# Moving the output products of a chunked scan into the next chunk, and the wide products that fill it into two places instead of three

## The chip, the cores and the metric

The kernel runs on one core of a Trainium2 chip. The metric is the device time of one execution in microseconds (us); 0.2% of it is 2.4 us. The engines are called as in the profile: PE (matrix products), PEld (the loading of the stationary operand for PE), DVE (VectorE), ACT (ScalarE), POOL (GpSimd) and SP (which here only issues DMAs). Each engine takes its instructions in the order in which the program put them into its queue.

## The reference, cut to what matters

One layer works on 512 tokens of width 1024, all in float32: a gated feed-forward half step, two token mixers side by side, a gated merge, a second half step and a last norm.

```python
x = x + 0.5 * swiglu(rms_norm(x, ffn1_norm), ffn1_w1, ffn1_w3, ffn1_w2)
p = rms_norm(x, mix_norm) @ w_in                    # columns of both mixers and of the two gates
y_a = rwkv7_mixer(token_shift(p[..., :SHIFT_COLS])) @ rwkv_proj
y_b = fox_mixer(p[..., SHIFT_COLS:SHIFT_COLS + FOX_COLS]) @ fox_proj
x = x + (sigmoid(g_a) * y_a + sigmoid(g_b) * y_b) @ w_out
x = x + 0.5 * swiglu(rms_norm(x, ffn2_norm), ffn2_w1, ffn2_w3, ffn2_w2)
out = rms_norm(x, final_norm)

def step(state, inp):                               # inside rwkv7_mixer: 8 heads of 64, over all 512 tokens
    r_t, w_t, k_t, v_t, a_t, b_t = inp
    sa = einsum('bhvk,bhk->bhv', state, a_t)
    state = state * w_t[:, :, None, :] + sa[..., :, None] * b_t[:, :, None, :] + v_t[..., :, None] * k_t[:, :, None, :]
    return state, einsum('bhvk,bhk->bhv', state, r_t)
```

The recurrence `step` is the part that the change is about. The second mixer, `fox_mixer`, is causal attention of 8 heads with a decay in its logits.

## The kernel before, in words

**Wide products.** A float32 weight tile is cut into a high and a low part: ACT casts the high part (L122, `whi`), DVE subtracts (L123, `wlo`). Each product with a 128 by 512 activation then takes three instructions on PE (L130, L131, L132). These "wide products" fill the two feed-forward blocks and the projections. A column of `w_in` takes 8 such triples, 24 instructions.

**The scan.** The recurrence is worked off in 16 chunks of 32 tokens (`NC` = 16). `step(p)` has prepared, per pair of heads, tiles `G` (decayed readers of the state), `BK` (writers) and, with a triangular inverse, `Tb`. A chunk `c` then has these parts, all small:
- `xps` (L781, 8 products): the state is read, in `R = Rs[c % 4]`. DVE copies the result to `Xs` (L784).
- `ups` (L788, 4 products): `Xs` through the chunk's inverse. ACT copies the result into `R`, four copies (L790, L791).
- `sps` (L795, 8 products): the new state from `R` and `Dt`. DVE multiplies by the decay into the next chunk's `Rn` (L797, two instructions). This ends the chain that chunk `c + 1` waits for.
- `yps` (L806, 8 products): the chunk's outputs, from `R` and `G`. ACT copies them to `V4` (L807). No later chunk needs them.
- every second chunk, `stage(c + 2)` brings in operands for two chunks: transposes `vp` and `bp` on PE, eight copies on ACT (L769, L770).

Each of the 8 products is two instructions in the trace.

**What fills the gaps.** Between dependent parts of a chunk PE has to wait for DVE or ACT. The list `holes` names, for successive triples of wide products, the small product behind which they are placed: `holes += [hx, hx, hu, hu, hs, hs]` puts two triples (six wide instructions) behind `xps`, two behind `ups` and two behind `sps`. The method `cols` takes its places from this list; the triples are those of the attention's query and key columns (`load_qk(2)` and `(3)`, tile `pq`) and of nine gate columns (`early`, tile `pgt`). `tc.issue_after` is the tool: it says that an instruction has to stand behind another on its queue.

**Attention.** It is written after the scan in the program and runs beside it: norms of queries and keys (`norm_qk`: L712, L142, L143, then PE L148 with tile `pq`, then L718, L719, L720), parts of queries and keys (L844 to L850), logits `lp` (L862 to L864), softmax (L870 to L876), transposes (L880, L882), products with values (L891, L893).

**What sets the order.** The order on every queue is made by a scheduler that plays the program through with its own costs when it is built. It moves whatever no `issue_after` or dependence holds. So a changed place on PE also changes the order on ACT, DVE, POOL and SP.

**Buffers.** `xps`, `yps`, `ups`, `sps`, `vp` and `bp` share three PSUM buffers in turn (pool `pr`). A new one of them can be written only when the one three places before it has been copied out.

Of the kernel before, what the change touches and what calls it, by code (L numbers as in the profile page):

```python
# [9 lines left out]
F32 = mybir.dt.float32  # L10
# [8 lines left out]
P = 128  # L19
# [6 lines left out]
NP = DA // P  # L26
C = 32
NC = T // C
# [23 lines left out]
def kernel(  # L52
# [7 lines left out]
    dve, act, pool, pe = nc.vector, nc.scalar, nc.gpsimd, nc.tensor  # L60
# [6 lines left out]
    pr = ctx.enter_context(tc.tile_pool(name="pr", bufs=3, space=PSUM))  # L67
# [358 lines left out]
    with ExitStack() as mx:  # L426
        rp = mx.enter_context(tc.tile_pool(name="rp", bufs=1))
        holes = []
        sctx = ExitStack()
        sp = sctx.enter_context(tc.tile_pool(name="sp", bufs=1))  # L430
        G = [[sp.tile([P, NC, 2, C], F32, name=f"G{p}{q}", tag=f"G{p}{q}") for q in range(2)] for p in range(NP)]
# [81 lines left out]
        V4 = rp.tile([P, NP, T], F32, name="V4", tag="V4")  # L513
# [149 lines left out]
        Tb = Tall[:].rearrange("p (a c t) -> p a c t", a=2, c=NC)  # L663
# [7 lines left out]
        def heads():  # L671
            return [(p, q) for p in range(NP) for q in range(2)]

        def half(q):
            return slice(q * 64, (q + 1) * 64)
# [72 lines left out]
        Rs, Ds = [RD[i // 2][:, i % 2] for i in range(4)], [RD[2 + i // 2][:, i % 2] for i in range(4)]  # L748
# [8 lines left out]
        def stage(c):  # L757
            vp = pr.tile([P, NP, 2, 64], F32, tag="b", name="vp")
            for p in range(NP):
                pe.transpose(vp[0:64, p].rearrange("p a b -> p (a b)"), vs[p][:, c * C:(c + 2) * C], ident[:])  # L760
            bp = pr.tile([P, NP, 2, 64], F32, tag="b", name="bp")
            for p in range(NP):
                pe.transpose(bp[:, p].rearrange("p a b -> p (a b)"),
                             BKs[p][:, c:c + 2].rearrange("p c a b -> p (c a b)"), ident[:])
            for j in range(2):
                Rj, Dj = Rs[(c + j) % 4], Ds[(c + j) % 4]
                for q in range(2):
                    o = 32 + (1 - q) * 64
                    act.copy(Rj[o:o + 32, :, q, :], vp[j * C:(j + 1) * C, :, q, :])  # L769
                    act.copy(Dj[half(1 - q), :, q, :], bp[half(j), :, q, :])  # L770

        stage(0)

        for c in range(NC):
            R, Rn, Dt = Rs[c % 4], Rs[(c + 1) % 4], Ds[c % 4]
            cs = slice(c * C, (c + 1) * C)
            xps = pr.tile([P, 2, 64], F32, tag="b", name="xps")
            for p, q in heads():
                o = (p // 2) * 64 + q * C
                with tc.issue_after(ahead.ins):  # L780
                    hx = pe.matmul(xps[o:o + C, p % 2, :], G[p][q][:, c, 0, :], R[:, p, q, :], start=True, stop=True,  # L781
                                   tile_position=(0, o))
            Xs = sp.tile([P, 2, 64], F32, tag="Xs", name="Xs", bufs=2)
            dve.tensor_copy(Xs[:], xps[:])  # L784
            ups = pr.tile([P, 2, 64], F32, tag="b", name="ups")
            for p in range(NP):
                h = half(p // 2)
                hu = pe.matmul(ups[h, p % 2, :], Tb[h, p % 2, c, :], Xs[h, p % 2, :], start=True, stop=True)  # L788
            for i in range(2):
                act.copy(R[64:96, 2 * i:2 * i + 2, 0, :], ups[64 * i:64 * i + 32])  # L790
                act.copy(R[0:32, 2 * i:2 * i + 2, 1, :], ups[64 * i + 32:64 * i + 64])  # L791
            if c + 1 < NC:
                sps = pr.tile([P, NP, 64], F32, tag="b", name="sps")
                for p, q in heads():
                    hs = pe.matmul(sps[half(q), p, :], Dt[:, p, q, :], R[:, p, q, :], start=True, stop=True)  # L795
                for q in range(2):
                    decay = dve.tensor_tensor(Rn[half(q), :, q, :], sps[half(q)],  # L797
                                      PC[half(q), :, c:c + 1].broadcast_to([64, NP, 64]), op=ALU.mult)
            holes += [hx, hx, hu, hu, hs, hs]
            if c == 0:  # L800
                begun = decay
            if c % 2 == 0 and c + 2 < NC:
                stage(c + 2)
            yps = pr.tile([P, NP, C], F32, tag="b", name="yps")
            for p, q in heads():
                pe.matmul(yps[half(q), p, :], R[:, p, q, :], G[p][q][:, c, 1, :], start=True, stop=True)  # L806
            act.copy(V4[:, :, cs], yps[:])  # L807

        aside = mx.enter_context(ExitStack())
        aside.enter_context(tc.issue_after(begun.ins))  # L810
# [24 lines left out]
        for p in range(NP):  # L835
# [5 lines left out]
            for q in range(2):  # L841
                h_, g_ = half(q), half(1 - q)
                h = 2 * p + q
# [8 lines left out]
            for i, bl in enumerate(((0, 1), (2,), (3,))):  # L852
# [33 lines left out]
                for j, b in enumerate(bl):  # L886
                    for k in range(b + 1):
                        o = at[b] + k * P
                        for q in range(2):
                            h = 2 * p + q  # L890
# [38 lines left out]
        for p in range(NP):  # L929
            y = vs[p]  # L930
# [140 lines left out]
```

## Time and profile before

| what | value |
| --- | --- |
| median of 3 runs | 1191.12 us (1190.68 to 1191.21) |
| the profiled execution | 1190.24 us |
| its span, first to last instruction | 1188.5 us |
| granted TensorE clock | 0.997 |
| PE busy | 1169.2 us, 98% of the span |
| DVE busy | 662.1 us, 56% |
| ACT busy | 457.1 us, 38% |
| the scan, from the first `xps` to the last `yps` | 550.8 to 715.65 us of the span |

The profiled execution lies 0.88 us under the median. The busy share of PE is modelled from the ends of overlapping matmuls: the start-to-start distance of two instructions is the better clock for it, and the prediction uses it.

### The profile page before, as it was taken

To read this page: it belongs to the slowest core of one execution; us is meant where nothing else is said; L and a number is where in the kernel's file an instruction comes from. 1 tells how busy PE (TensorE), PEld (TensorE's weight loads), DVE (VectorE), ACT (ScalarE), POOL (GpSimd) and SP (SyncE) were. 2 spreads that over 40 slices of the span, in tenths; PEclk is the share of its full clock that TensorE was granted. 3 is DMA by queue.
4 is the path that set the end of the run, shared out by engine and by line. 5 is a ranking of instruction groups with operands and counts; after the bars stand their busy time and mean duration, and the time that the engine had idled before them with its cause. 6 is when DMAs were issued, how large, how long until landed. Compare 5 with 4: busy or idle time off the path is not lost.

```text
span 1188.5 us, 15870 instructions
## 1 busy us (share of the span) xinstructions
PE 1169.2 (98%) x6334; PEld 952.3 (80%) x6334; DVE 662.1 (56%) x993; ACT 457.1 (38%) x739; POOL 100.4 (8%) x144
## 2 busy tenths in 40 slices
PE   8999999999999999999999999999999999999997
PEld 7888888888887888887767777778888888888887
DVE  6555545443444888686766657866545545543242
ACT  6322222222223855346776756524222222222221
POOL 4200000001111112401000011121000000000110
PEclk9999999999999999999999999999999999999999
DMA  7333333323333433344212135633333333323331
GB/s 200 89 91 104 89 106 89 103 83 115 116 116 96 121 108 111 111 124 116 55 46 87 55 99 175 193 100 107 89 98 98 90 105 91 104 80 98 98 98 72
DMA packets 208152, 122.54 MB, mean 103 GB/s; under 512 B 9902, under 2 KB 200430, under 8 KB 208078
## 3 DMA queue, kind: packets, MB, share of 16 engines
q1 hardware_dynamic: 202078, 108.67, 31.8%
q0 software_dynamic: 3760, 12.06, 3.2%
q8 instruction: 50, 0.82, 0.3%
q10 hardware_dynamic: 2240, 0.79, 0.3%
q14 instruction: 24, 0.20, 0.1%
HBM read 110.82 MB, written 10.68 MB: 102 GB/s over the span
## 4 chain that ended last, share of the span: by engine, by line
PE 95%; DVE 3%; ACT 1%; DMA 1%; issue 0%; POOL 0%; SPq 0%; DVEq 0%; POOLq 0%
PE pd L131 7%; PE pd L130 7%; PE pd L132 7%; PE pa L132 7%; PE pa L131 7%; PE pb L131 7%; PE pb L132 7%; PE pa L130 7%; PE pb L130 7%; PE pgt L130 3%; PE pgt L132 2%; PE pgt L131 2%; PE pk L130 2%; PE pk L132 2%; PE pk L131 2%; PE pw L132 1%
## 5 line engine op out<-in xcount | busy, mean ns | idle before, releaser
L122 ACT CAST whi<-raw 128x1024 fp32r<-128x1024 f32 (+2 forms) x197 | 196.4, 998 | 605.9 <-PE pa L131 175.5
L123 DVE TENSOR_TENSOR wlo<-raw,whi 128x1024 fp32r<-128x1024 f32 (+2 forms) x197 | 227.5, 1155 | 129.1 <-ACT whi L122 129.0
L132 PE MATMUL pa<-xh,wlo 128*128 128x512 f32 x344 | 133.9, 389 | 0.0
L131 PE MATMUL pa<-xl,whi 128*128 128x512 f32 x344 | 133.8, 389 | 0.0
L132 PE MATMUL pb<-xh,wlo 128*128 128x512 f32 x344 | 133.8, 389 | 0.0
L130 PE MATMUL pa<-xh,whi 128*128 128x512 f32 x344 | 133.8, 389 | 0.0
L130 PE MATMUL pb<-xh,whi 128*128 128x512 f32 x344 | 133.8, 389 | 0.0
L131 PE MATMUL pb<-xl,whi 128*128 128x512 f32 x344 | 133.8, 389 | 0.0
L132 PE MATMUL pd<-hh,wlo 128*128 128x512 f32 x330 | 129.0, 391 | 0.0
L131 PE MATMUL pd<-hl,whi 128*128 128x512 f32 x330 | 128.5, 389 | 0.0
L130 PE MATMUL pd<-hh,whi 128*128 128x512 f32 x330 | 128.4, 389 | 0.0
L350 DVE TENSOR_TENSOR fb<-pb,rstd 128x512 f32<-128x512 f32 x43 | 29.7, 691 | 137.2 <-PE pb L132 137.2
L130 PEld LDWEIGHTS pa<-xh,whi 128*128 128x128 f32 x344 | 64.6, 188 | 13.5
L132 PEld LDWEIGHTS pb<-xh,wlo 128*128 128x128 f32 x344 | 64.6, 188 | 13.4
L131 PEld LDWEIGHTS pb<-xl,whi 128*128 128x128 f32 x344 | 64.6, 188 | 13.5
L132 PEld LDWEIGHTS pa<-xh,wlo 128*128 128x128 f32 x344 | 64.5, 188 | 13.5
L131 PEld LDWEIGHTS pa<-xl,whi 128*128 128x128 f32 x344 | 64.6, 188 | 13.4
L130 PEld LDWEIGHTS pb<-xh,whi 128*128 128x128 f32 x344 | 64.5, 188 | 13.4
L131 PEld LDWEIGHTS pd<-hl,whi 128*128 128x128 f32 x330 | 61.9, 188 | 12.9
L132 PEld LDWEIGHTS pd<-hh,wlo 128*128 128x128 f32 x330 | 62.0, 188 | 12.7
L130 PEld LDWEIGHTS pd<-hh,whi 128*128 128x128 f32 x330 | 62.0, 188 | 12.7
L346 DVE TENSOR_TENSOR fa<-pa,rstd 128x512 f32<-128x512 f32 x43 | 29.7, 691 | 68.5 <-PE pa L132 68.4
(397 smaller groups left out, 1964.5 us busy)
## 6 DMA issues: line engine op xcount, KB each, us to landing
raw<-in_ffn_w_dram SPq DMA_DIRECT2D x116, 512.0 KB
raw<-in_w_in_dram SPq DMA_DIRECT2D x40, 512.0 KB
raw<-in_ffn_w_dram SPq DMA_DIRECT2D x15, 384.0 KB
raw<-in_w_out_dram SPq DMA_DIRECT2D x8, 512.0 KB
gsave<-gs SPq DMA_DIRECT2D x9, 256.0 KB
xin<-in_x_dram SPq DMA_DIRECT2D x4, 512.0 KB
xsave<-xT POOLq DMA_DIRECT2D x8, 256.0 KB, 2.3
G<-gsave POOLq DMA_DIRECT2D x8, 256.0 KB, 3.8
```

Source lines behind the costliest of these rows:

```text
L122: act.copy(hi[:], raw[:])
L123: (eng or dve).tensor_tensor(lo[:], raw[:], hi[:].bitcast(F32), op=ALU.subtract)
L130: pe.matmul(ps, whi, xhi, start=first, stop=False)
L131: pe.matmul(ps, whi, xlo, start=False, stop=False)
L132: return pe.matmul(ps, wlo, xhi, start=False, stop=last)
L346: dve.tensor_tensor(a[:], pa[:], nrm.rstd[:], op=ALU.mult)
L350: dve.tensor_tensor(b[:], pb[:], nrm.rstd[:], op=ALU.mult)
```

## The change

The output products `yps` of chunk `c` move from the end of chunk `c` to chunk `c + 1`, between that chunk's `xps` and `ups`. A new function `outputs` holds them. Each of the three parts `xps`, `yps`, `ups` is tied behind the one before it by `issue_after`. The six triples of a chunk are now placed three behind `ups` and three behind `sps`, none behind `xps`. In chunk 0 there is no earlier output, so `ups` follows `xps` directly.

```diff
+        def outputs(c, behind):
+            yps = pr.tile([P, NP, C], F32, tag="b", name="yps")
+            with tc.issue_after(behind.ins):
+                for p, q in heads():
+                    y = pe.matmul(yps[half(q), p, :], Rs[c % 4][:, p, q, :], G[p][q][:, c, 1, :], start=True, stop=True)
+            act.copy(V4[:, :, c * C:(c + 1) * C], yps[:])
+            return y
...
             dve.tensor_copy(Xs[:], xps[:])
+            if c:
+                hx = outputs(c - 1, hx)
             ups = pr.tile([P, 2, 64], F32, tag="b", name="ups")
             for p in range(NP):
                 h = half(p // 2)
-                hu = pe.matmul(ups[h, p % 2, :], Tb[h, p % 2, c, :], Xs[h, p % 2, :], start=True, stop=True)
+                with tc.issue_after(hx.ins):
+                    hu = pe.matmul(ups[h, p % 2, :], Tb[h, p % 2, c, :], Xs[h, p % 2, :], start=True, stop=True)
...
-            holes += [hx, hx, hu, hu, hs, hs]
+            holes += [hu] * 3 + [hs] * 3
...
-            yps = pr.tile([P, NP, C], F32, tag="b", name="yps")
-            for p, q in heads():
-                pe.matmul(yps[half(q), p, :], R[:, p, q, :], G[p][q][:, c, 1, :], start=True, stop=True)
-            act.copy(V4[:, :, cs], yps[:])
+        outputs(NC - 1, hu)
```

In the changed kernel the lines below the new function are 7 to 10 higher: `yps` is L776 (its copy L777), `xps` L788, `Xs` L791, `ups` L798, the copies behind it L800 and L801, `sps` L805, the decay L807; `norm_qk` keeps its numbers.

On PE, at chunk 1, this stands before (the rows are: line, operation, tile written, tiles read, shape):

```order
L781 MATMUL xps<-RD_4261,G_2720 32x64
L130 MATMUL pq<-xh_2606,whi 128x512
L131 MATMUL pq<-xl_2607,whi 128x512
L132 MATMUL pq<-xh_2606,wlo 128x512
L130 MATMUL pq<-xh_2700,whi 128x512
L131 MATMUL pq<-xl_2701,whi 128x512
L132 MATMUL pq<-xh_2700,wlo 128x512
L788 MATMUL ups<-Xs,Tall 64x64 x4
```

and this stands there now:

```order
L788 MATMUL xps<-RD_4261,G_2720 32x64
L776 MATMUL yps<-G_2713,RD_4261 64x32
L776 MATMUL yps<-G_2714,RD_4261 64x32
L776 MATMUL yps<-G_2715,RD_4261 64x32
L776 MATMUL yps<-G_2716,RD_4261 64x32
L776 MATMUL yps<-G_2717,RD_4261 64x32
L776 MATMUL yps<-G_2718,RD_4261 64x32
L776 MATMUL yps<-G_2719,RD_4261 64x32
L776 MATMUL yps<-G_2720,RD_4261 64x32
L148 MATMUL pq_5090<-shi,bonesr 128x512
L798 MATMUL ups<-Xs,Tall 64x64 x4
```

The six wide products between `xps` and `ups` are gone; the outputs of chunk 0 stand there, and one product of `norm_qk`, which reads the cast `shi`.

On ACT, the difference at the same place, between the copies of chunk 0's `ups` and those of chunk 1's (`nf` is the attention's decay, `vp` and `bp` the staging transposes, `qsq` and `shi` what `norm_qk` needs for L148):

```order
+L823 ACTIVATE nf<-nf,onec 8x512
 L769 COPY RD_4262<-vp 32x4x64 x4
-L816 ACTIVATE nf<-nf,onec 8x512
 L770 COPY RD_4264<-bp 64x4x64 x4
 L712 ACTIVATE qsq<-qk_4133 128x512
-L807 COPY V_2881<-yps 128x4x32
-L122 CAST whi<-raw 128x1024
-L142 CAST shi<-qsq 128x512
```

The logarithm `nf` now stands ahead of the staging copies; behind `qsq` the difference goes on with the new lines `L777 COPY V` and `L142 CAST shi`, and the weight cast L122 has moved further back.

On DVE, the difference between the decay of chunk 0 and the copy `Xs` of chunk 1 (`klc` and `qa` are parts of keys and queries):

```order
+L855 TENSOR_TENSOR klc_5078<-qk_4100,kb_5119 64x512
+L852 TENSOR_TENSOR qa_5117<-qk_4067,qa_5117 64x512
+L807 TENSOR_TENSOR RD_4261<-sps,PC 64x4x64 x2
 L708 TENSOR_TENSOR qk_4133<-qk_4133,rstd 128x512
 L708 TENSOR_TENSOR qk_4166<-qk_4166,rstd 128x512
-L845 TENSOR_TENSOR qa_5117<-qk_4067,qa_5117 64x512
-L848 TENSOR_TENSOR klc_5078<-qk_4100,kb_5119 64x512
```

Two instructions have moved ahead of the decay (L807 now, L797 before), on which the next chunk's `xps` waits.

More of the change, by code (lines that the diff above doesn't have):

```diff
@@ L775 @@
             R, Rn, Dt = Rs[c % 4], Rs[(c + 1) % 4], Ds[c % 4]
-            cs = slice(c * C, (c + 1) * C)
             xps = pr.tile([P, 2, 64], F32, tag="b", name="xps")
```

## The prediction

> **What bounds the kernel now.** First the page: busy time by engine, and the chain of work that ended last.
>
> ```profile
> PE 1169.2 (98%) x6334; PEld 952.3 (80%) x6334; DVE 662.1 (56%) x993; ACT 457.1 (38%) x739; POOL 100.4 (8%) x144
> PE 95%; DVE 3%; ACT 1%; DMA 1%; issue 0%; POOL 0%; SPq 0%; DVEq 0%; POOLq 0%
> ```
>
> PE is busy 98% of the span and makes 95% of the chain. So a change is worth what it does to the start-to-start distances on PE, and nothing else. Next the windows before, during and after the scan, to see how much room is there (PE busy, PEld, DVE, ACT, POOL).
>
> ```profile
> 350.00:550.00 200.00, 200.00 (x1096) 162.02 (x1095) 141.71 (x221) 96.57 (x135) 34.04 (x61) 1.00 0.42 114
> 550.00:716.00 166.00, 160.19 (x1601) 120.92 (x1600) 110.31 (x240) 118.89 (x299) 6.04 (x11) 1.00 0.24 68
> ```
>
> PE idles 166.00 - 160.19 = 5.8 us in the scan and not at all before it. ACT is busy 72% of the scan and DVE 66%, so neither bounds it as a whole; but both may be late at a place. The granted clock is 1.00, so the throttle is out of it. Third, PE's timeline, for where it idles: time, duration, and the idle time in front with its releaser.
>
> ```profile
> 559.64 0.45 PE L781 MATMUL xps<-RD,G 128*32 128x64 f32 x16 [0.71 <-ACT RD L769]
> 562.79 0.46 PE L788 MATMUL ups<-Xs,Tall 64*64 64x64 f32 x8 [1.12 <-ACT V L807]
> 569.14 0.44 PE L781 MATMUL xps<-RD,G 128*32 128x64 f32 x14 [0.19 <-DVE RD L797]
> 610.82 0.30 PE L862 MATMUL lp<-kb,qa 128*128 128x128 f32 x1 [1.18 <-ACT qrn L719]
> 612.43 0.46 PE L788 MATMUL ups<-Xs,Tall 64*64 64x64 f32 x8 [0.77 <-DVE Xs L784]
> 671.89 0.33 PE L862 MATMUL lp<-kb,qa 128*128 128x128 f32 x1 [1.11 <-DVE qk L893]
> 676.05 0.33 PE L862 MATMUL lp<-kb,qa 128*128 128x128 f32 x1 [0.29 <-ACT tr L882]
> ```
>
> These seven waits sum to 5.37 us: 2.02 in chunks 1 and 2, 3.35 in chunks 6 and 12. They hang on the queues of ACT and DVE, and the change reorders both.
>
> **The change, part by part.** *The trips between wide and small products.* The timeline at chunks 9 and 15 has their price.
>
> ```profile
> 639.80 0.66 PE L806 MATMUL yps<-G,RD 128*64 128x32 f32 x16
> 640.39 0.44 PE L781 MATMUL xps<-RD,G 128*32 128x64 f32 x16
> ...
> 711.11 0.39 PE L131 MATMUL pgt<-xl,whi 128*128 128x512 f32 x1
> 711.34 0.39 PE L132 MATMUL pgt<-xh,wlo 128*128 128x512 f32 x1
> 711.66 0.46 PE L788 MATMUL ups<-Xs,Tall 64*64 64x64 f32 x8
> 712.04 0.50 PE L130 MATMUL pgt<-xh,whi 128*128 128x512 f32 x1
> 712.38 0.39 PE L131 MATMUL pgt<-xl,whi 128*128 128x512 f32 x1
> 712.61 0.40 PE L132 MATMUL pgt<-xh,wlo 128*128 128x512 f32 x1
> ```
>
> Wide products follow each other after 0.23 us. The last one before `ups` takes 0.32 (711.34 to 711.66): 0.09 more. The first one after it takes 0.34 to its successor (712.04 to 712.38): 0.11 more. The eight instructions of `ups` take 0.38 until the next wide one; about 0.12 of that is the leaving, if I read it like the other pair: 16 instructions of `yps` take 0.59 to `xps`, of which I put 15 steps of 0.03 at 0.44 and the change of shape at 0.15, that is 0.12 over a step. So a trip costs 0.09 + 0.12 + 0.11 = 0.32 us, and a change of shape among small ones 0.12. Two chunks, one with staging, had six trips (`xps` / `ups` / `sps` with staging / `yps` and `xps` / `ups` / `sps` with `yps` interleaved) and one change of shape. They now have four trips (`xps`, `yps`, `ups` together / `sps`, twice) and four changes. Saved: 2 x 0.32 - 3 x 0.12 = 0.28 per pair, times 8 pairs: 2.2 us. By a count of the places where attention's products now stand otherwise I allow 1.4 to 3.0. The products themselves stay the same in number.
>
> [...] If every change of shape cost alike, 13 per pair (staging's aside) would become 12, and 8 x 0.12 = 1.0 us would be saved in place of 2.2.
>
> *The waits that go.* The waits at 559.64 to 569.14, measured start to start, cost 0.79 + 1.18 + 0.43 = 2.4 us (one can lose a little more than its idle time, as the end of a matmul is modelled). The later four cost 1.2 + 0.84 + 1.13 + 0.27 = 3.4. Whether they come back is asked next.
>
> *The waits that come, chunks 0 to 2.* In chunk 0 nothing stands between `xps` and `ups`. ACT and DVE at chunks 0 and 1:
>
> ```profile
> 551.08 1.22 DVE L123 TENSOR_TENSOR wlo<-raw,whi 128x1024 fp32r<-128x1024 f32 x1 [3.96 <-ACT whi L122]
> 552.22 0.28 DVE L784 COPY Xs<-xps 128x128 f32<-128x128 f32 x1
> 557.27 0.86 DVE L797 TENSOR_TENSOR RD<-sps,PC 64x256 f32<-64x256 f32 x2
> ...
> 558.11 1.48 ACT L769 COPY RD<-vp 32x256 f32<-32x256 f32 x4
> 559.62 0.72 ACT L816 ACTIVATE nf<-nf,onec 8x512 f32<-8x512 f32 x1
> 560.36 1.50 ACT L770 COPY RD<-bp 64x256 f32<-64x256 f32 x4
> 561.88 0.63 ACT L712 ACTIVATE qsq<-qk 128x512 f32<-128x512 f32 x1
> 562.53 0.27 ACT L807 COPY V<-yps 128x128 f32<-128x128 f32 x1
> 562.70 1.05 ACT L122 CAST whi<-raw 128x1024 fp32r<-128x1024 f32 x1
> 563.64 0.62 ACT L142 CAST shi<-qsq 128x512 fp32r<-128x512 f32 x1
> ```
>
> `xps` of chunk 0 began at 550.82; `Xs` is copied from 552.22, behind a weight subtraction that is the same in both kernels. PE could start `ups` at 551.3 and starts it at 552.5: **1.2 us**. At chunk 1, PE goes through 18 wide products and the staging and is at `xps` at about 559.5, which is also where the decay comes (DVE now has `klc` and `qa` ahead of it, so 558.1 + 1.4). Then `yps`, done at 560.9. Next on PE is L148, which reads `shi`. ACT's queue ahead of `shi` is full without a gap: the copies of `bp` end at 561.86, L712 at 562.5, `V` at 562.8, and `shi`, no longer behind L122, at 563.4. So L148 waits from 560.9 to 563.4: **2.5 us**, and `ups` stands behind it. At chunk 2 two L148 stand between `yps` and `ups`. The second reads `slo`, for which DVE's rows are:
>
> ```profile
> 565.24 1.22 DVE L818 TENSOR_TENSOR_SCAN la<-onesr,nf 8x512 f32<-8x512 f32 x1
> 567.22 0.87 DVE L824 CAST klc<-la 8x512 fp32r<-8x512 f32 x2
> 568.11 0.88 DVE L797 TENSOR_TENSOR RD<-sps,PC 64x256 f32<-64x256 f32 x2
> 569.02 1.38 DVE L827 TENSOR_TENSOR klc<-la,klc 8x512 fp32r<-8x512 f32 x2
> 570.43 0.69 DVE L143 TENSOR_TENSOR slo<-qsq,shi 128x512 fp32r<-128x512 f32 x1
> 571.93 0.75 DVE L720 SCALAR_TENSOR_TENSOR qk<-qk,par,qrn 128x512 f32<-128x512 f32 x1
> ```
>
> From `Xs` of chunk 1 at 563.3 DVE now runs `slo` 0.7, the scan 1.2, `klc` 0.9 and 1.4, `slo` 0.7, two of 0.7 and 0.4, a weight subtraction 1.2, the decay 0.9, L720 twice 1.5, a small maximum 0.3 and this `slo` 0.7, 10.6 us together: `slo` comes at about 574. PE, after 18 wide products, two sets of logits and `yps`, is there at 572.7 or so: **1.3 us**. The sum is 1.2 + 2.5 + 1.3 = 5.0 us (3.5 to 6.0) against 2.4 before.
>
> *The waits that come, chunks 3 to 15.* `yps` alone covers 0.15 + 0.45 + 0.15 = 0.75 us between `xps` and `ups`, where six wide products covered 1.7. The copy `Xs` itself needs about 0.5. In all these chunks but one the order puts products of attention (transposes, value products or logits) beside `yps` as well, which brings the cover to 1.2 to 2.1 us. Adding up DVE's queue between `xps` and `Xs` for chunks 4, 6, 9 and 11 I find it just in time each time. The logits at 610.82 and 671.89, which waited for queues of ACT and DVE, now stand behind nine wide products in place of six, 0.7 us later. I take 0.5 us here, with bounds 0 and 3.4, the whole of what those four cost before.
>
> *The other queues.* POOL gets two gate loads ahead of one that waited before; they are wanted two chunks later. SP gets the fourth weight tile of `fox_proj` behind the load of `lgsave`, which waits for the last `yps`; it is issued some 4 us later and wanted 42 wide products after that `yps`, 9.6 us. I take nothing for both; without the cover the second costs up to 1 us. The longer hole behind `ups` and `sps` hides ACT's and DVE's copies better, which took nothing from PE beyond the rows above.
>
> **The sum.** -2.2 (trips) - 2.4 - 3.4 (waits that go) + 5.0 + 0.5 (waits that come) = -2.5 us. Against the profiled execution's own 1190.24 us that is 1187.7; the median of the runs is 0.88 higher, so I forecast 1191.12 - 2.5 = **1188.6 us**.
>
> **The rivals.** *The copy `Xs` comes as late as before, without its cover (slower).* DVE's copies do not follow `xps` at once, as chunks 4 and 14 show:
>
> ```profile
> 588.47 0.44 PE L781 MATMUL xps<-RD,G 128*32 128x64 f32 x16
> 590.56 0.28 DVE L784 COPY Xs<-xps 128x128 f32<-128x128 f32 x1
> 591.18 0.46 PE L788 MATMUL ups<-Xs,Tall 64*64 64x64 f32 x8
> 697.56 0.28 DVE L784 COPY Xs<-xps 128x128 f32<-128x128 f32 x1
> 697.89 0.45 PE L788 MATMUL ups<-Xs,Tall 64*64 64x64 f32 x8
> ```
>
> Chunk 4 had 591.18 - 590.84 = 0.34 us to spare, chunk 14 0.05. With a cover 1.0 us shorter and DVE as late as before, the first waits 0.7 and the second 1.0, and so on, some 0.3 a chunk over chunks 3 to 15: 4 us. If the logits also wait as before for 2.4, the sum is -2.2 - 5.8 + 5.0 + 4 + 2.4 = +3.4: 1194.5 us. Against it: the scheduler has filled the hole with attention's products again. It decides once the waits of `ups` pass 3 us in all. Chance 0.23.
>
> *The later waits return in other places (no change).* Then 3.4 take the place of 0.5, and the sum is +0.4: 1191.5. For it: the logits depend on long runs of DVE and ACT work that stay as long. Or a joint of two shapes costs as much as leaving for wide products does, and the trips save 1.0 in place of 2.2: 1189.8. For that speaks the 0.15 from `yps` to `xps`, against it the 0.09 and 0.11 that only wide neighbours show. Together 0.22, a third of it for the second. [...] *ACT's queue bites less than I think.* If L148 of chunk 1 waits 1 us in place of 2.5 and the trips save 3.0, the result is 1186.3. It is in the forecast's chance, 0.55 together.
>
> **How the numbers follow.** 0.2%, 2.4 us, is about what a measurement of this kernel can tell from no change. The forecast (0.55) counts as faster; its own range, with the bounds of the trips, of the early waits and 1 us of late ones, is 1186 to 1189.5. The rival of returning waits gives the middle 0.22, the late `Xs` the 0.23 of slower. The range has to reach into both: 1185.8 to 1193.6.
>
> **What would show it.** In the changed kernel's PE timeline: `ups` of chunk 0 waits 1.2 us for `Xs`; L148 waits over 2 us for ACT's `shi` ahead of chunk 1's `ups`; a second L148 over 1 us at chunk 2; after that no wait over 0.5 us. From `ups` of chunk 3 to the last `yps` PE must be 4 to 5 us shorter than before (3.4 - 0.5 of waits, and some 1.7 of trips). The forecast is wrong if `ups` waits for `Xs` in most chunks (the slower rival), or if the idle sum after chunk 3 is again over 3 us (no change).

## The result, and the profile after

The changed kernel takes 1195.95 us (median of 4 runs, 1194.56 to 1197.24), the kernel before 1190.90 us beside it (4 runs, 1189.08 to 1191.21). The ratio is 1.0044, with a 95% interval of 1.0031 to 1.0056: slower by 5 us, where 2.5 us less was forecast. The time lies above the range, which ended at 1193.6. The profiled execution took 1194.56 us, its span is 1192.8 us (before 1188.5).

The page of the changed kernel, busy time by engine and the chain that ended last:

```profile
PE 1169.2 (98%) x6334; PEld 955.2 (80%) x6334; DVE 664.5 (56%) x993; ACT 457.6 (38%) x739; POOL 100.2 (8%) x144
...
PE 91%; DMA 2%; issue 2%; DVE 2%; ACT 2%; POOL 0%; SPq 0%; DVEq 0%; POOLq 0%; ACTq 0%
```

PE's busy time is what it was, to the tenth; its share of the chain fell from 95% to 91%. PE's timeline shows the waits (start, duration, and in brackets the idle time in front with its releaser):

```profile
551.05 0.52 PE L798 MATMUL ups<-Xs,Tall 64*64 64x64 f32 x8 [1.30 <-DVE Xs L791]
558.15 0.45 PE L788 MATMUL xps<-RD,G 128*32 128x64 f32 x16 [0.22 <-DVE RD L807]
558.77 0.66 PE L776 MATMUL yps<-G,RD 128*64 128x32 f32 x16 [0.17 <-ACT RD L769]
561.76 0.49 PE L148 MATMUL pq<-shi,bonesr 128*128 128x512 f32 x1 [2.33 <-ACT shi L142]
...
572.53 0.40 PE L148 MATMUL pq<-slo,bonesr 128*128 128x512 f32 x1
...
608.95 0.46 PE L798 MATMUL ups<-Xs,Tall 64*64 64x64 f32 x8 [0.23 <-DVE Xs L791]
620.25 0.33 PE L869 MATMUL lp<-kb,qa 128*128 128x128 f32 x1 [1.90 <-ACT tr L889]
643.68 0.46 PE L798 MATMUL ups<-Xs,Tall 64*64 64x64 f32 x8 [0.66 <-DVE Xs L791]
675.75 0.46 PE L798 MATMUL ups<-Xs,Tall 64*64 64x64 f32 x8 [0.57 <-DVE Xs L791]
698.12 0.46 PE L798 MATMUL ups<-Xs,Tall 64*64 64x64 f32 x8 [1.41 <-DVE Xs L791]
752.97 0.73 PE L130 MATMUL ppj<-ya,whi 128*128 128x512 f32 x2 [1.66 <-ACT ya L154]
756.46 0.50 PE L130 MATMUL ppj<-ya,whi 128*128 128x512 f32 x1 [1.56 <-ACT whi L122]
```

The forecast waits of chunks 0 and 1 are there almost to the tenth (1.30 for 1.2, 2.33 for 2.5); that of chunk 2 is not (572.53 starts without one). After chunk 2 come 0.23, 1.90, 0.66, 0.57 and 1.41, and 0.25 for the logits at 672.00, where 0.5 in all was forecast: together 5.02. From `ups` of chunk 3 to the last `yps` PE was to be 4 to 5 us shorter; it takes 134.01 us (582.22 to 716.23) in place of 133.62 (581.37 to 714.99). At 752.97 a wait has grown that is far behind the scan: it was 0.75 us before. There PE waits for `ya`, the normalized output of the first mixer, which the projection `ppj` reads.

The second thing is the clock. The windows view of the changed kernel, in stretches of 3.41 us (length, PE busy, PEld, DVE, ACT, POOL, granted clock, share of DMA, GB/s):

```profile
559.08:562.49 3.41, 1.08 (x22) 0.73 (x18) 3.25 (x6) 2.54 (x7) 0.00 (x0) 1.00 0.00 0
562.49:565.90 3.41, 3.41 (x14) 2.65 (x10) 3.29 (x6) 2.94 (x7) 0.00 (x0) 0.50 0.00 0
617.10:620.51 3.41, 1.51 (x28) 1.23 (x22) 1.91 (x4) 3.36 (x8) 0.00 (x0) 1.00 0.02 5
620.51:623.93 3.42, 3.42 (x18) 2.73 (x18) 1.02 (x5) 2.29 (x9) 0.00 (x0) 0.50 0.81 230
753.63:757.05 3.42, 1.85 (x8) 1.04 (x7) 1.91 (x4) 3.29 (x6) 0.00 (x0) 1.00 0.72 270
757.05:760.46 3.41, 3.41 (x9) 2.72 (x9) 3.18 (x6) 2.30 (x4) 0.00 (x0) 0.50 0.48 145
```

Three times a stretch in which PE was busy for only 1.08, 1.51 or 1.85 us is followed by one in which the granted clock is 0.50 (half clock, below). The edges lie on one grid (its stretches are called grid stretches below): 620.51 is 17 stretches after 562.49, and 757.05 is 40 after that. In such a stretch the wide products go slower, as PE's timeline shows at chunk 1:

```profile
563.19 0.63 PE L131 MATMUL pq<-xl,whi 128*128 128x512 f32 x1
563.61 0.63 PE L132 MATMUL pq<-xh,wlo 128*128 128x512 f32 x1
564.04 0.63 PE L130 MATMUL pq<-xh,whi 128*128 128x512 f32 x1
```

They follow each other after 0.43 us, elsewhere after 0.23. The profiled execution of the kernel before had none of this between its first 14 us and its last 4: a mean clock of 0.997, against 0.993 in this execution and 0.989 to 0.991 in the other three of the changed kernel.

One row of the windows view for each kernel gives the balance, from the first `xps` to the first product with `w_out` (L130, tile `pw`), the same PE work in both. Before:

```profile
550.82:770.29 219.47, 211.35 (x1813) 160.68 (x1813) 153.66 (x308) 152.16 (x355) 14.28 (x26) 1.00 0.33 99
```

After:

```profile
549.31:774.61 225.30, 212.78 (x1814) 164.58 (x1814) 154.35 (x308) 152.55 (x355) 14.45 (x26) 0.98 0.31 96
```

The stretch is 5.83 us longer. Length less PE busy is waiting: 8.12 us before, 12.52 after, 4.40 more. The busy time holds both the half clock and the trips; the experiments take them apart. (The span differs by only 4.3: the kernel before came to its first `xps` 1.5 us later in this execution, and its clock was halved from 10.45 to 13.87 us, where that of the changed kernel was not.)

### The profile page after: what moved, and what is told of

It reads as the page before. It is cut to its first block, busy times and chain, and to the rows that moved or that the text cites. A ratio compares the mean times of both kernels' runs of the same rounds, so it can differ in the third digit from the quotient of the medians.

```text
span 1192.8 us, 15868 instructions
## 1 busy us (share of the span) xinstructions
PE 1169.2 (98%) x6334; PEld 955.2 (80%) x6334; DVE 664.5 (56%) x993; ACT 457.6 (38%) x739; POOL 100.2 (8%) x144
## 4 chain that ended last, share of the span: by engine, by line
PE 91%; DMA 2%; issue 2%; DVE 2%; ACT 2%; POOL 0%; SPq 0%; DVEq 0%; POOLq 0%; ACTq 0%
PE pd L131 7%; PE pd L130 7%; PE pd L132 7%; PE pa L132 7%; PE pb L132 7%; PE pb L130 7%; PE pa L130 7%; PE pb L131 7%; PE pa L131 7%; PE pgt L130 2%; PE pgt L131 2%; PE pgt L132 2%; PE pk L130 2%; PE pk L132 2%; PE pk L131 2%
## 5 line engine op out<-in xcount | busy, mean ns | idle before, releaser
L122 ACT CAST whi<-raw 128x1024 fp32r<-128x1024 f32 (+2 forms) x197 | 196.2, 998 | 604.1 <-PE pa L131 176.0
L130 PE MATMUL pa<-xh,whi 128*128 128x512 f32 x344 | 134.0, 389 | 0.0
L130 PE MATMUL pb<-xh,whi 128*128 128x512 f32 x344 | 133.9, 389 | 0.0
L130 PE MATMUL pd<-hh,whi 128*128 128x512 f32 x330 | 128.6, 390 | 0.0
L130 PEld LDWEIGHTS pb<-xh,whi 128*128 128x128 f32 x344 | 64.6, 188 | 13.4
L130 PEld LDWEIGHTS pa<-xh,whi 128*128 128x128 f32 x344 | 64.6, 188 | 13.3
L131 PEld LDWEIGHTS pd<-hl,whi 128*128 128x128 f32 x330 | 62.0, 188 | 12.8
L130 PEld LDWEIGHTS pd<-hh,whi 128*128 128x128 f32 x330 | 62.0, 188 | 12.7
```

What stands on the lines that cost most here:

```text
L122: act.copy(hi[:], raw[:])
L130: pe.matmul(ps, whi, xhi, start=first, stop=False)
L131: pe.matmul(ps, whi, xlo, start=False, stop=False)
```

## Experiments

The theory to test: the loss is waits, and stretches of half clock that the waits bring. The rivals: the clock is beside the point; or the trips between wide and small products save nothing; or one of the two parts of the change is the loss.

**Does a wait bring half clock? Ten pauses in a stage that is otherwise full.** To the kernel before, at ten places of the second feed-forward block (`dl` is a tile of 128x1024 bf16; `tie` places the column's wide products behind the pause; `range(1)` is w_one, w_two has 2 and w_three 3):

```diff
+    def pause(ps, last):
+        with tc.issue_after(last.ins):
+            a = pe.matmul(ps[:, 0:64], identb[:], dl[:, 0:64], start=True, stop=True)
+        for _ in range(1):
+            pool.memset(dl[:], 0.0)
...
+        with tc.issue_after(a.ins):
+            return pe.matmul(ps[:, 0:64], identb[:], dl[:, 0:64], start=True, stop=True)
...
+                        gap = final and w is w1 and j in range(2, 21, 2)
+                        tie = [pause(ps, end)] * KD if gap else [end] * KD if end else []
...
```

> The kernel before, with ten pauses of PE in the second feed-forward block, which is otherwise wide products without a gap: ahead of every second pair of columns a small product reads a tile, POOL clears it once (128x1024), and the next small product, behind which all wide products of the column are tied, reads it again. Estimate from POOL's rows (a clearing of 128x1024 took 1.22 us): 1.0 to 1.5 us of idle time at each place. Theory (half clock for 3.41 us follows a stretch of 3.41 us with about 1.6 us or more of idle time): no half clock, 10 x 1.5 us more than before: 1203 to 1207. Rival (the clock doesn't hang on such waits): the same.

> The same ten pauses, each with two clearings by POOL: 2.0 to 2.7 us of idle time. Theory: where the pause lies in the fixed grid of 3.41 us decides; at 2.3 us some 7 of 10 pauses put 1.6 us into one stretch, so 5 to 9 stretches of half clock in the block at 1.7 us each, 8 to 15 us on top of ten waits: 10 x (w_one's price + 1.0) + 12, 1222 to 1232. Rival (the clock doesn't hang on such waits): 10 us more than w_one, no half clock, 1213 to 1218.

> The same ten pauses, each with three clearings by POOL: 3.0 to 4.0 us of idle time. Theory: every pause puts 1.6 us or more into a stretch, so at least ten stretches of half clock, some twice: 17 to 25 us on top of the waits, 10 us of waits more than w_two: 1238 to 1252. Rival: 10 us more than w_two's waits alone, no half clock: 1223 to 1229.

The medians are 1206.06, 1218.40 and 1237.52 us (4 runs each), against 1190.69 before. From w_one to w_two the time rises by 12.3, from w_two to w_three by 19.1, while each step adds 10.1 us of waiting: the idle times are 1.13, 2.13 and 3.14 us at a place, 11.2, 21.3 and 31.4 in all. w_one's profile has no half clock in the block, w_two's has one stretch, w_three's seven. The theory's limit of 1.6 us was too low for this block: w_two fell short of the 1222 expected and lies next to the rival's 1218, and w_three just short of 1238. It is w_three that decides: the rival had 1229 at most. PE's timeline of w_three at the first three pauses:

```profile
839.98 0.19 PE L349 MATMUL pa<-dl,identb 128*128 128x64 bf16 x1 [3.09 <-POOL dl L344]
...
865.22 0.19 PE L349 MATMUL pa<-dl,identb 128*128 128x64 bf16 x1 [3.14 <-POOL dl L344]
...
892.09 0.19 PE L349 MATMUL pa<-dl,identb 128*128 128x64 bf16 x1 [3.14 <-POOL dl L344]
```

From the first to the second it takes 25.24 us, from the second to the third, with a half-clock stretch (865.88 to 869.30) behind the second, 26.87. Work and pause are the same: one stretch costs 1.63 us. And the windows of w_three show where the limit lies in this block:

```profile
917.08:920.50 3.42, 1.54 (x8) 1.29 (x8) 2.80 (x4) 0.00 (x0) 1.77 (x2) 1.00 0.21 58
1022.89:1026.31 3.42, 1.49 (x7) 1.24 (x7) 2.85 (x4) 0.00 (x0) 1.82 (x2) 1.00 0.15 44
```

After the first, with 1.88 us idle, the clock stayed; after the second, with 1.93, it was halved. In w_two the one stretch with 2.01 us idle is the one that was followed by half clock:

```profile
959.07:962.48 3.41, 1.40 (x7) 1.19 (x7) 3.27 (x5) 0.73 (x1) 1.90 (x2) 1.00 0.00 0
962.48:965.89 3.41, 3.41 (x10) 2.62 (x9) 0.14 (x1) 0.00 (x0) 0.00 (x0) 0.50 0.53 154
```

At the other places of w_two the grid cuts the pause in two, so that no stretch has more than 1.85 us idle, and no half clock follows.

**The same pauses, filled.** w_three with eight wide products inside each pause:

```diff
+        for _ in range(8):
+            with tc.issue_after(a.ins):
+                a = pe.matmul(ps[:], onesr[:], nrm2.hi[0][:], start=True, stop=True)
```

> w_three with eight more wide products (results never used) inside each of the ten pauses, between the two small products: the pause lasts as long, since the second small product still waits for POOL's three clearings, but only about 1.3 us of it is idle. Theory (the idle time within a stretch decides): no half clock in the block, so the seven to ten stretches of half clock of w_three go and the pauses stay: 1224 to 1228, against 1237.5. Rival (the waits alone make the time): 1236 to 1238 as w_three.

1225.33 us (4 runs, 1224.93 to 1225.98): as expected, 12.2 us less than w_three, with 80 products more. The second small product comes no sooner, but PE idles only 1.19 us in front of it:

```profile
867.25 0.19 PE L349 MATMUL pa<-dl,identb 128*128 128x64 bf16 x1 [1.19 <-POOL dl L344]
```

The block has no half clock. The rival falls: the same pause costs less when PE is kept at work.

**The changed kernel with fillers at its two longest waits.** The L148 that waited in chunk 1 is tied behind `fill[1]`, the logits of chunk 7 behind `fill[7]`:

```diff
             if c:
                 hx = outputs(c - 1, hx)
...
+            if c in (1, 7):
+                for _ in range(6):
+                    with tc.issue_after(hx.ins):
+                        hx = pe.matmul(up[:, 0:T], bonesr[:], mix.hi[0][:], start=True, stop=True)
+                fill[c] = hx
...
-        norm_qk(1)
+        norm_qk(1, fill[1])
...
```

> The changed kernel with six more wide products (128x512, results never used) on PE between the output products and the inverse product of chunks 1 and 7, where PE waited 2.33 and 1.90 us and a stretch of half clock of 3.41 us followed each time; the waiting products are tied behind the six. Theory (the stretches of half clock are the loss): 6 x 0.23 = 1.4 us of the wait is filled, the idle time left at each place is under 1.2 us, no half clock follows in 559 to 570 us nor after chunk 7, and the time falls by two stretches at about 1.6 us, 3 us: near 1193 (1191.5 to 1194.5). Rival (the waits themselves are the loss, the clock is beside it): the fillers only occupy time that PE waited, 1196 as the changed kernel, up to 0.5 more.

1193.23 us (11 runs, 1190.75 to 1194.13), against 1191.28 before; ratio 1.0015 (1.0007 to 1.0024). As expected: 2.7 us under the changed kernel, with 12 products more, and no half clock in the scan (behind it, from 752.60, the profile has two stretches at the wait for `ya`, one more than the changed kernel's). What is left of the two waits (a wait for a PSUM buffer ahead of the fillers, and one for the logits):

```profile
561.45 1.67 PE L802 MATMUL ups<-xh,bonesr 128*128 128x512 f32 x6 [0.86 <-ACT RD L772]
620.20 0.33 PE L879 MATMUL lp<-kb,qa 128*128 128x128 f32 x1 [0.45 <-ACT tr L899]
```

**The waiting products tied behind `ups`.** `hus[1]` and `hus[7]` are the last inverse products of chunks 1 and 7; the first logits of chunk 7 are tied behind the second:

```diff
+                with tc.issue_after(behind.ins) if behind else ExitStack():
+                    summed(ps[:], bonesr, parts)
...
-        norm_qk(1)
+        norm_qk(1, hus[1])
...
```

> The changed kernel with the two products that waited (the first product of norm_qk(1) in chunk 1, the logits of the second pair in chunk 7) tied behind their chunk's inverse product. Both theories: the waits of 2.33 and 1.90 us shrink, by 2 to 4 us together, some of it coming back at the later place. Theory (half clock is the loss): the two stretches of half clock go as well, 3 us more: 1189.5 to 1191.5. Rival (waits alone): 1192 to 1194.

A miss for both: 1197.12 us (5 runs). PE's timeline and DVE's show that the wait of chunk 1 did not shrink:

```profile
563.46 0.70 PE L801 MATMUL ups<-Xs,Tall 64*64 64x64 f32 x8 [2.52 <-DVE Xs L794]
```

```profile
560.86 0.69 DVE L859 TENSOR_TENSOR klc<-qk,kb 64x512 fp32r<-64x512 f32 x1
561.59 0.69 DVE L856 TENSOR_TENSOR qa<-qk,qa 64x512 fp32r<-64x512 f32 x1
562.30 0.68 DVE L828 SCALAR_TENSOR_TENSOR nf<-la,nf 8x512 f32<-8x512 f32 x1
563.02 0.29 DVE L794 COPY Xs<-xps 128x128 f32<-128x128 f32 x1
```

With `shi` out of the way `ups` itself waits, 2.52 us, for `Xs`, which stands behind attention's operations on DVE. In the changed kernel the same operations stand ahead of `Xs`, which is copied from 561.51 there; the L148 that waits for `shi` starts at 561.76. In chunk 1 two queues are late at once, and the prediction named only ACT's. The windows view, from the first `xps` to the first product with `w_out` again, tells the theory from the rival:

```profile
550.81:777.53 226.72, 215.39 (x1814) 165.69 (x1813) 154.46 (x308) 152.06 (x355) 14.44 (x26) 0.96 0.31 95
```

PE waits 11.33 us, 1.19 less than in the changed kernel, and the stretch is 1.42 us longer all the same: five stretches are at half clock where the changed kernel has three. By the waits alone it would be shorter.

**Each part of the change alone.** Outputs moved, three places as before (`hy` is the last output product):

```diff
-            holes += [hu] * 3 + [hs] * 3
+            holes += [hy, hy, hu, hu, hs, hs]
```

> One part alone: the output products moved as in the changed kernel, but the wide products in three places again (two triples behind the outputs, two behind the inverse product, two behind the new state). Theory: the waits of chunks 0 to 2 are covered by wide products, no idle stretch reaches 1.8 us, so no half clock in the scan; the trips are as many as before and a joint of shapes comes to it, so about 2 to 3 us more than a changed kernel without half clock (about 1190.5): 1192 to 1193.5. Rival (joints and trips cost alike and little): 1190 to 1191. Rival (the moved outputs are the loss): 1195 or more.

1194.57 us (6 runs, 1192.40 to 1195.99), ratio 1.0030 (1.0017 to 1.0042): between the theory and the third rival. The same stretch in its windows view:

```profile
550.02:773.50 223.48, 213.87 (x1814) 163.14 (x1813) 154.01 (x308) 152.07 (x355) 14.34 (x26) 0.98 0.32 97
```

It waits 9.61 us, 1.5 more than before, and has two stretches of half clock. The theory had said that wide products in the old places keep every idle stretch short; they didn't: `ups` waits 1.73 and 2.16 us for `Xs` at 642.92 and 675.81. Half clock follows the first; the grid cuts the second in two. The other stretch of half clock lies behind the scan, after a wait of 1.94 us at 718.16 for the normalization's `yqa`.

And two places, with the outputs where they were, in the kernel before:

```diff
-            holes += [hx, hx, hu, hu, hs, hs]
+            holes += [hu] * 3 + [hs] * 3
```

> The other part alone: the kernel before with the wide products in two places (three triples behind the inverse product, three behind the new state), the output products where they were, at the chunk's end. Theory: the inverse product follows the state reading with only attention's products between; what the outputs cover in the changed kernel, 0.6 us a chunk, comes on top as waits for Xs, 3 to 6 us of idle time more than the changed kernel's 9 in the scan, with half clock where it gathers: 1196 to 1203. Rival (places matter only through trips): as the changed kernel without half clock, 1190 to 1192.

```profile
550.01:784.07 234.06, 217.41 (x1813) 167.58 (x1813) 153.69 (x308) 151.41 (x355) 14.37 (x26) 0.96 0.31 92
```

1204.01 us (4 runs), a little above the range: 16.65 us of waits and six stretches of half clock. So neither part alone gains: the moved outputs lose 3.3 us against the kernel before, and the two places 12.8, which the moved outputs bring down to 5.

**The load behind the scan.** SP's timeline before (time of issue, and count):

```profile
702.58 10.75 SPq L110 DMA_DIRECT2D raw<-in_fox_proj_dram  x2
```

and after, with the cast on ACT that reads the weight tile:

```profile
704.94 0.38 SPq L110 DMA_DIRECT2D raw<-in_fox_proj_dram  x1
716.84 0.32 SPq L928 DMA_DIRECT2D G<-lgsave  x1
718.68 1.41 SPq L110 DMA_DIRECT2D raw<-in_fox_proj_dram  x2
```

```profile
726.50 0.62 ACT L122 CAST whi<-raw 128x512 fp32r<-128x512 f32 x1 [4.00 <-DMA raw<-in_fox_proj_dram]
727.03 1.08 ACT L942 ACTIVATE G<-yc 128x512 f32<-128x512 f32 x2
```

One weight tile now stands behind the load of `lgsave` (a saved tile of the first mixer's gate), which waits for the last `yps`. ACT waits 4.00 us for it, and the squares of the normalization (L942) stand behind that cast. The experiment moves those loads to POOL's queue:

```diff
-        nc.sync.dma_start(lg[0:96, :], lgsave[:])
+        nc.gpsimd.dma_start(lg[0:96, :], lgsave[:])
...
-            nc.sync.dma_start(bons[p], bsave[p])
+            nc.gpsimd.dma_start(bons[p], bsave[p])
```

> The changed kernel with the loads of lgsave and bsave issued by POOL in place of SP, so that SP's loads of fox_proj weights do not stand behind a load that waits for the last outputs; the scan's order is that of the changed kernel. Theory: the cast of the third weight tile no longer waits for its load (4.00 us of ACT's idle time at 726.5), the norm's squares behind it come 3 us earlier, PE's wait for ya falls from 1.66 to 0.75 us or less and its 0.24 at 727 goes: 1.1 us less, and 1.6 less again in the executions where that wait brought a stretch of half clock: 1193 to 1195. Rival (the wait for ya hangs on the normalization's own chain, not on the load): 1196, the wait is still 1.6.

1191.97 us (11 runs, 1191.43 to 1194.27), ratio 1.0010 (1.0001 to 1.0019). ACT no longer waits for the load, and PE's wait for `ya` is the 0.75 of before:

```profile
751.47 0.73 PE L130 MATMUL ppj<-ya,whi 128*128 128x512 f32 x2 [0.75 <-ACT ya L154]
```

In its windows view the stretch is 3.00 us shorter than after, 1.08 of it waits. The other 1.92 are PE's busy time, and here only two stretches are at half clock: the third is gone. (A stretch of wide products cost 1.63 above. The first two lie 1.1 us later here; whether that is the rest isn't shown.)

```profile
549.44:771.74 222.30, 210.86 (x1814) 163.22 (x1814) 154.25 (x308) 152.83 (x355) 16.98 (x31) 0.98 0.33 97
```

The stretch ahead of the third one idles by the wait of 1.56 us at 756.46, which the kernel before has too (1.57 at 753.51) without half clock behind it. But the late load goes with it: the three profiles in which `ya` waits 1.66 us (after, a_fill, b_tied) have half clock at this place, the eight in which it waits 0.75 have none.

The median fell by 4.0, more than expected; the executions of the changed kernel with a mean clock of 0.989 and 0.990 had more half clock than the profiled one.

**Both repairs.** Fillers and the moved loads together:

> The changed kernel with both repairs: six fillers each in chunks 1 and 7, and the loads of lgsave and bsave issued by POOL. Theory: no half clock in the scan, the wait for ya 0.75 us as before, and the trips' gain of 2 to 3 us stands: the fillers took 2.7 us off the changed kernel and the loads 4.0, some of it shared by chance: 1189 to 1190.5, 1 to 2 us under before. Rival (the trips save nothing and what is left are waits): 1191.5 to 1193.

```profile
550.93:770.44 219.51, 211.61 (x1825) 163.90 (x1825) 154.10 (x308) 152.13 (x355) 17.04 (x31) 1.00 0.32 99
```

1189.23 us (11 runs, 1188.68 to 1190.78), against 1190.69 before (15 runs); ratio 0.9989 (0.9980 to 0.9997). By the medians it beats both kernels: 1.5 us under the one before, 6.7 under the changed kernel. The granted clock is 1.00 through the whole stretch. Less 12 fillers at 0.23 = 2.76, PE works 208.85 us in it, before 211.35: **the trips save 2.5 us**, an estimate, since it takes the fillers off at 0.23 each. In the profiled executions the stretch is no shorter than before (219.51 us, before 219.47): the fillers take what the trips save. So the 1.5 us of the medians lie between executions that were not profiled, and where they come from isn't shown.

Work that is needed in place of fillers, in chunks 0, 1 and 7, with the moved loads:

```diff
+            holes += [hy, hy, hu, hu, hs, hs] if c in (0, 1, 7) else [hu] * 3 + [hs] * 3
```

> The changed kernel with lgsave and bsave loaded by POOL, and in chunks 0, 1 and 7 the wide products in three places (two triples between outputs and inverse product) in place of fillers. Theory: the waits of 1.3, 2.3 and 1.9 us fill with work that is needed, so up to 4 us less idle time than e_load_pool and no half clock in the scan, for three trips more (1 us): 1187.5 to 1189.5. Rival (the waits come back at the next place where ACT and DVE are late, as in b_tied): 1190 to 1193.

```profile
551.55:770.35 218.80, 209.28 (x1813) 161.15 (x1813) 154.26 (x308) 152.94 (x355) 16.94 (x31) 1.00 0.33 99
```

1189.87 us (11 runs, 1188.59 to 1192.32), against 1191.25; ratio 0.9993 (0.9984 to 1.0003). No half clock in the scan, PE busy 209.28, which is 2.07 less than before without a filler to take off, and with three trips more than the changed kernel; but it waits 9.52 us, so a part came back elsewhere, as the rival said. The median lies between the two expectations, and it can't be told from the kernel before.

## Why the prediction was wrong

The balance of 5.83 us can now be divided; the busy time's part of it, by f_both. Trips: 208.85 - 211.35 = -2.50. Half clock: 212.78 - 208.85 = +3.93, three stretches at 1.31 (1.63 where all of it is wide products). Waits: +4.40. The sum is +5.83, where the forecast had -2.2 for trips, nothing for half clock and -0.3 for waits, -2.5 in all. So two steps failed: half clock was put at nothing (3.9 of the difference), and the waits were taken too small (4.7).

- **The trips (-2.2): right.** 2.5 by f_both, 2.07 by g_mixed with three trips more, and none in c_moved_three_places, which has as many trips as before: 213.87 less two stretches at an estimated 1.31 is 211.25, before 211.35. So what was read from the timeline's rows held as a sum; single trips weren't measured. The rival, by which every change of shape costs alike, would have left 1.0. The joint from `yps` to `xps`, put at 0.15 us from the timeline of before (639.80 to 640.39), did not eat the gain.
- **"The granted clock is 1.00, so the throttle is out of it": the first step that failed.** The clock of the kernel before (0.997 in its profile) did not tell that of the changed kernel (0.993), which waits otherwise. The prediction itself put a wait of 2.5 us behind 1.4 us of small products at chunk 1, and priced it as 2.5; it cost 2.33, all in one grid stretch (559.08 to 562.49), and then a stretch of half clock (562.49 to 565.90). The kernel before had idled at most 1.57 us in one grid stretch (751.14 to 754.55) between its first 17 us and its last 10, and no half clock followed; in w_three's block 1.93 us were enough.
- **Waits that come after chunk 2 (0.5, bounds 0 to 3.4): the second step that failed, mis-sized.** They came to 5.02. I had added up DVE's queue for chunks 4, 6, 9 and 11 and carried "just in time" to the others. It did not even hold for the four: chunks 6 and 9 wait 0.23 and 0.66. Chunks 7, 12 and 14 I had not added up. The 1.90 of chunk 7 came from ACT:

```profile
617.80 1.28 ACT L682 ACT_TABLE_LOAD   x1
619.09 0.63 ACT L682 ACTIVATE gs<-gs 128x512 f32<-128x512 f32 x1
619.63 0.57 ACT L889 COPY tr<-lp 128x512 f32<-128x512 f32 x1
```

  A table load and a gate stand ahead of the copy `tr` for which PE waits; in the changed kernel no wide products stand there to cover it. The rival "the later waits return in other places" described this, without its clock.
- **Chunks 0 and 1 (1.2 and 2.5): right in size,** 1.30 and 2.33. Chunk 1's cause was only half right: b_tied showed that DVE is as late as ACT. (The prediction itself had `Xs` at 563.3 there and `shi` at 563.4.) **Chunk 2 (1.3): wrong,** no wait. DVE came about when I had reckoned; but PE reached that product 23.2 us after the scan's start (572.53 - 549.31), where I had 21.9 (572.7 - 550.8), since chunk 1 had run at half clock.
- **"I take nothing" for SP: wrong.** I said that without the cover it costs up to 1 us. The cover, 42 wide products, was counted on PE; on ACT there was none, since the normalization's squares stood behind the cast. It cost 1.08 us of waits (e_load_pool without it), and in this execution a stretch of half clock, some 1.6 to 1.9.
- **The late `Xs` (the slower rival)** was to decide by waits of `ups` over 3 us. They sum to 1.30 + 0.23 + 0.66 + 0.57 + 1.41 = 4.2, so by its own sign it was right that the kernel is slower. But 1.30 is chunk 0, which the forecast had; over chunks 3 to 15, where the rival had 4, they are 2.87 in four chunks, not in most. The kernel before had 0.77 there, so its cause is 2.1 us of the 5.83. It was right on chunk 14 (1.41, where it had 1.0): there `Xs` stands on DVE behind a gate that POOL loads,

```profile
696.45 0.69 DVE L974 TENSOR_TENSOR ga<-ga,rstd 128x512 f32<-128x512 f32 x1 [3.67 <-DMA ga<-gsave]
```

  a wait that the kernel before has too (2.71 us), with six wide products on PE to cover it. Whether the changed order of POOL's loads, for which the prediction took nothing, made it longer isn't shown.

## What to carry to other kernels

A wait of PE had two prices in these runs: its length, and a stretch of half clock, which followed all 15 grid stretches with 1.90 us or more of idle time and 9 of the 31 with 1.45 to 1.89 us; so sum the idle time over stretches of 3.41 us. Cover taken out of a loop must be checked in each turn of the loop, for each queue that ends there, and a load that moves behind a waiting one must be followed to the instruction that stands behind its reader. Where one or two turns are late, fill those and keep the better order for the rest: with the load moved as well, that made a kernel that lost 5 us into one that is 1.5 under the kernel before, by the medians.

## What the runs showed of the hardware

In the profiles of before, after and the eleven experiments, at full clock and between the first 15 us and the last 10, all 15 grid stretches in which PE idled for 1.90 us or more were followed by half clock; of 31 with 1.45 to 1.89 us, 9 were; of those with less, one (1.36 us, among small products). In w_three's block the edge lies between 1.88 and 1.93 us. Elsewhere it was lower: among the wide products behind the scan 1.57 us was enough in the changed kernel (753.63 to 757.05), while the same wait brought no half clock in eight other profiles. So idle time is not all that counts; what is counted stays open. Behind a stretch that was itself at half clock, the next was so with less: after 0.72, 0.79 and 0.89 us of idle time, once each. The same waits can fall either way on the grid. w_three_filled has the scan of the kernel before, whose waits of 1.18 and 0.77 us at chunk 6 brought no half clock; in w_three_filled they (1.17 and 0.77) fell into one grid stretch, and it followed:

```profile
609.19:612.60 3.41, 1.50 (x15) 1.28 (x16) 3.29 (x7) 1.99 (x6) 0.00 (x0) 1.00 0.00 0
612.60:616.01 3.41, 3.41 (x11) 2.17 (x11) 3.09 (x9) 1.92 (x5) 0.00 (x0) 0.50 0.00 0
```

That this is also what moves the mean clock of the kernel before from execution to execution (0.995 to 0.998 in 22 of them) fits, but wasn't profiled.
